# A three-layer block on one core with its opening rebuilt: squares and seven modulation slabs on TensorE, the shift added into FFN 0's operand, filter arithmetic on VectorE, another load order

## The chip, the cores and the metric

One core of one Trainium2 chip. The engines are TensorE (PE, its weight loads PEld), VectorE (DVE), ScalarE (ACT), GpSimd (POOL) and SyncE (SP), which issues nearly all loads. The metric is the device time of one execution in microseconds, of which the median of the runs is given. Rows of the trace count from the start of the span of the one profiled execution.

## The reference

A sequence of 256 tokens of width 1024 passes two layers and a third one of another kind. Each of the first two is an FFN, a mixer and a second FFN, and each of these three has a shift, a gain and a gate that come from a conditioning vector c through a matrix of 1024 by 9216:

```python
cond = jax.nn.silu(c)
for l in range(DEPTH):
    m = (cond @ w_mod[l] + b_mod[l]).reshape(bsz, 3, 3, D_MODEL)
    x = x + 0.5 * m[:, 0, 2][:, None] * swiglu(adaln_in(x, norm_g[l, 0], m, 0), ...)   # FFN 0
    h = adaln_in(x, norm_g[l, 1], m, 1) @ w_in[l]
    ...                                   # mixer_ab (layer 0), mixer_cd (layer 1)
    x = x + m[:, 1, 2][:, None] * (mix @ w_out[l])
    x = x + 0.5 * m[:, 2, 2][:, None] * swiglu(adaln_in(x, norm_g[l, 2], m, 2), ...)
def adaln_in(x, g, m, i):
    return rmsnorm(x, g) * (1 + m[:, i, 1][:, None]) + m[:, i, 0][:, None]
```

`mixer_cd` in layer 1 needs the spectrum of a long filter: three small layers of 64 with a sine, a product with `f_w4`, a decay, and a transform of 512 points. It depends on no token, so it can be computed at any time before layer 1's mixer. Layer 0 needs none of it.

## The kernel before

Everything is fp32. x lies in SBUF with the 1024 features on partitions, as 8 pieces of 128 x 256 tokens. A large product is done with each operand split in a rounded high part and a low part (fp32r), so one 128x128 block costs three matmuls: high by high, high by low, low by high. A slab is one 128 x 1024 piece of weights (512 KB): 8 blocks, 24 matmuls, 128 outputs for 256 tokens. FFN 0 reads 43 slabs of its first two matrices (the first three together, block by block, as x's pieces come), then 22 slabs for the projection down.

Weights and the modulation matrix come in one stream of 512 KB loads, in the order of the list `order`: `("w", i)` is a weight slab, `("m", i)` a modulation slab. They land in a ring of 6 buffers (u_75 to u_80); a load waits until the work that read its buffer is done. For a weight slab ACT rounds the high part and VectorE subtracts it to get the low part, into a ring of 5 pairs (u_81/u_82 to u_89/u_90). For a modulation slab VectorE multiplies 128 rows by the silu of c (`condb`, c repeated on all partitions) and sums each row: one column of `mods` (u_70). Slabs 0 to 7 hold the gain of layer 0's FFN 0, slabs 8 to 15 its shift. In the kernel before slabs 8 to 11 are instead laid out for TensorE (`PE_GROUPS`): products with a weight of one column, 512 columns streamed, a copy, and four more matmuls that turn the row into columns.

The order on each engine is written by a planner: jobs ask for an engine, and the one that can start soonest by its own costs is placed next, with penalties (`HPEN` for the filter's job, `RPEN`, `MPEN`, ...). What is in an engine's queue then runs strictly in that order. Tiles of one program differ by number (u_127 to u_129: PSUM of the slabs; u_130 to u_134: PSUM for the rest; u_68, u_69: high and low part of the normalised x).

The opening before: c is spread over partitions by two matmuls; x's squares are made by ACT, added up by POOL and summed over partitions by TensorE (`Norm.square`, `Norm.root`); then a reciprocal root of eight small VectorE operations (`rsqrt`), a spread over partitions by TensorE (`spread`), and `normalise`: x times gain times root, split in high and low part. FFN 0's shift rides along as two further columns of the operand (258 instead of 256), filled by `shift_cols`, and is added as a bias when a slab is read out (`done`). `hyena_spectrum` runs beside all this, with its additions on POOL (`reduce_angle`, `tap_sums`). The jobs of the opening have to end before the mixer of layer 0 begins: `main` waits for `bg` after FFN 0.

Of the kernel before, what the change touches and what calls it, by code (L numbers as in the profile page):

```python
# [11 lines left out]
F32 = mybir.dt.float32  # L12
# [3 lines left out]
ALU = mybir.AluOpType  # L16
# [4 lines left out]
P = 128  # L21
# [114 lines left out]
PE_GROUPS = (2,)  # L136
# [4 lines left out]
def _pack(inp):  # L141
# [79 lines left out]
    for l in range(2):  # L221
        m = np.ascontiguousarray(inp["w_mod"][l].T).reshape(9, 8, P, 1024)
        m = m[M_SECS].reshape(18, 4, P, 1024)
        if l == 0:
            for g in PE_GROUPS:
                o = M_SECS[g // 2] * D + g % 2 * 512
                m[g] = inp["w_mod"][0][:, o:o + 512].reshape(4, 2, P, 512).transpose(0, 2, 1, 3).reshape(4, P, 1024)
        ms.append(m.reshape(72, P, 1024))
# [67 lines left out]
EX = (2, 3, 8)  # L296
DRATE, DLAT = 350.0, 1.3
HPEN = -0.6
# [178 lines left out]
def _body(tc, ins, out, ctx, dbg=None):  # L477
# [74 lines left out]
    order = [("m", i) for i in range(12)] + [("w", 0)] + [("m", i) for i in range(12, 16)]  # L552
    mi, credit = 16, 0.0
    for i in range(NW):
        if i:
            order.append(("w", i))
# [8 lines left out]
    m_ev = {(l, s): Event() for l in range(2) for s in range(9)}  # L565
    cond_ev, x_ev = Event(), Event()
# [31 lines left out]
    def lo_job():  # L598
        for oi, (kind, i) in enumerate(order):
# [11 lines left out]
            elif i // 4 in PE_GROUPS:  # L611
                continue
            else:
# [8 lines left out]
                mod_done(l, M_SECS[r // 8], 1)  # L622
# [4 lines left out]
    def mod_done(l, s, n):  # L627
        m_left[l, s] = m_left.get((l, s), 8) - n
        if m_left[l, s] == 0:
            fire(m_ev[l, s])  # L630


    def pe_mod(g, ccol, one1, row):
        c0 = M_SECS[g // 2] * 8 + g % 2 * 4
        yield cond_ev
        b, = yield chb, 1
        for i in range(4):
            oi = order.index(("m", 4 * g + i))
            yield raw_ev[oi]
            yield "pe"  # L640
            for e in range(2):
                k = 2 * i + e
                pe.matmul(b[0:1], ccol[:, k:k + 1], raw_t[oi][:, 512 * e:512 * e + 512], start=(k == 0), stop=(k == 7))
            put(raws, raw_t.pop(oi))
        yield "act"
        act.activation(row, b[0:1], AF.Copy)
        put(chb, b)
        b, = yield chb, 1
        yield "pe"
        for j in range(4):  # L650
            pe.matmul(b[:, j:j + 1], row[:, j * P:j * P + P], one1[:, 0:1], start=True, stop=True)
        yield "dve"
        dve.tensor_tensor(mods[0][:, c0:c0 + 4], b[:, :4], V("b_mod", c0, 4), ALU.add)
        put(chb, b)
        mod_done(0, M_SECS[g // 2], 4)
# [140 lines left out]
    class Norm:  # L796
        def __init__(self, A, h, lo, width=D):
# [5 lines left out]
            self.adder = ("dve", dve)  # L803
# [17 lines left out]
        def normalise(self, k, src):  # L821
# [4 lines left out]
            yield from split(self.h[:, k, :T], self.lo[:, k, :T], t, self.need(k))  # L826
            put(sc, t)
            self.use()
# [7 lines left out]
        def square(self, src):  # L836
# [5 lines left out]
            else:  # L842
                yield self.adder[0]
                self.adder[1].tensor_tensor(self.acc, self.acc, s, ALU.add)
# [5 lines left out]
        def root(self):  # L850
            b, = yield chb, 1
            r, = yield sm, 1
            if self.rows:
                self.rstd, = yield sc, 1
# [3 lines left out]
            put(sc, self.acc)  # L858
            yield from rsqrt(r[:, :2], b[:, :2], self.width, sm, (chb, b))
# [87 lines left out]
    def ffn(l, i, nm, nxt):  # L947
        with tc.tile_pool(name=f"ffn{l}{i}", bufs=1) as sp:
# [5 lines left out]

            def done(s, ps):
                t, = yield sc, 1
                b, = yield sm, 1
                if nm.whole:
                    h = ps[:, :T]
                    yield "act"  # L960
                    act.activation(b[:, 0:1], ps[:, T:T + 1], AF.Copy)
                else:
                    h = t
                    yield from evict(nm, t, b[:, 0:1], ps)
                j = s // 2
                if s == 42:
# [4 lines left out]
                    if nm.whole:  # L971
                        put(mmr, ps)
# [5 lines left out]
                elif s % 2 == 0:  # L978
                    yield "act"
                    act.activation(t, h, AF.Silu, bias=b[:, 0:1])  # L980
                    if nm.whole:
                        put(mmr, ps)
# [1362 lines left out]
```

## Time and profile before

| what | value |
|---|---|
| runs of the kernel before | 1431.0, 1426.72, 1430.66 us; median 1430.66 us |
| profiled execution | 1425.9 us, of which the span is 1424.0 us |
| PE busy, share of the span | 1375.6 us, 97% |
| VectorE, ScalarE, GpSimd | 80%, 55%, 3% |
| FFN 0's slabs begin | first matmul at 55.35 us, without larger gaps from 57.74 us |

The busy shares are means over the whole span. In the opening PE has gaps, while behind it the matmuls follow each other almost without one. A PE time in a row of matmuls is modelled at its end; the start of the next weight load or matmul is the surer mark.

### The profile page before, as it was taken

To read this page: it belongs to the slowest core of one execution; us is meant where nothing else is said; L and a number is where in the kernel's file an instruction comes from. 1 tells how busy PE (TensorE), PEld (TensorE's weight loads), DVE (VectorE), ACT (ScalarE), POOL (GpSimd) and SP (SyncE) were. 2 spreads that over 40 slices of the span, in tenths; PEclk is the share of its full clock that TensorE was granted. 3 is DMA by queue.
4 is the path that set the end of the run, shared out by engine and by line. 5 is a ranking of instruction groups with operands and counts; after the bars stand their busy time and mean duration, and the time that the engine had idled before them with its cause. 6 is when DMAs were issued, how large, how long until landed. Compare 5 with 4: busy or idle time off the path is not lost.

```text
span 1424.0 us, 26962 instructions
## 1 busy us (share of the span) xinstructions
PE 1375.6 (97%) x10726; PEld 1292.5 (91%) x10726; DVE 1141.8 (80%) x2183; ACT 778.2 (55%) x1434; POOL 40.9 (3%) x44
## 2 busy tenths in 40 slices
PE   5899999999999999999999999999999999999998
PEld 1499999878999999999998789999998779899998
DVE  5788788796888777888979879986577878799962
ACT  2365554474555544555447646655455765576642
POOL 5200000000000000000000001000000000000000
PEclk9999999999999999999999999999998999899999
DMA  8678889754787776888974447676643244366671
GB/s 296 220 252 315 290 311 326 241 160 152 248 264 249 239 246 226 299 272 279 343 283 152 158 146 231 221 253 184 192 143 107 72 130 138 90 184 186 193 228 54
DMA packets 84655, 305.25 MB, mean 214 GB/s; under 512 B 9515, under 2 KB 11147, under 8 KB 84274
## 3 DMA queue, kind: packets, MB, share of 16 engines
q1 hardware_dynamic: 83250, 299.31, 64.5%
q0 software_dynamic: 1280, 4.22, 0.9%
q8 instruction: 84, 1.38, 0.4%
q14 instruction: 41, 0.34, 0.1%
HBM read 302.43 MB, written 1.06 MB: 213 GB/s over the span
## 4 chain that ended last, share of the span: by engine, by line
PE 84%; DVE 7%; ACT 5%; DMA 1%; POOL 1%; issue 1%; SPq 0%; ACTq 0%; DVEq 0%; POOLq 0%
PE u L445 84%; DVE u L445 7%; ACT u L445 4%; POOL u L445 1%; DMA u<-wst 1%; DMA u<-x 1%; ACT L445 0%; SPq L572 0%; POOL u L2151 0%; ACTq L445 0%; DVEq L445 0%; DVE u L1655 0%; DVE u L1159 0%; DVE u L1656 0%; DVEq L1159 0%
## 5 line engine op out<-in xcount | busy, mean ns | idle before, releaser
L445 PE MATMUL u<-u,u 128*128 128x258 f32 (+7 forms) x10724 | 1374.5, 292 | 44.7 <-ACT u L445 24.2
L445 PEld LDWEIGHTS u<-u,u 128*128 128x128 f32 (+3 forms) x10724 | 1292.2, 189 | 126.1 <-issue 50.3
L445 ACT ACTIVATE u<-u 128x1024 fp32r<-128x1024 f32 (+6 forms) x1001 | 603.1, 632 | 534.0 <-PE u L445 311.3
L445 DVE TENSOR_TENSOR u<-u,u 128x1024 fp32r<-128x1024 f32 (+5 forms) x1065 | 734.0, 721 | 181.0 <-ACT u L445 91.9
L445 DVE SCALAR_TENSOR_TENSOR u<-u,u,u 128x256 f32<-128x256 f32 (+2 forms) x393 | 185.6, 481 | 65.2 <-PE u L445 34.2
L445 ACT ACTIVATE u<-u,u 128x256 f32<-128x256 f32 (+2 forms) x323 | 165.3, 523 | 85.6 <-DVE u L445 61.0
L445 DVE CUSTOM_DVE_ANT_0 u<-u,u,u 128x1024 f32<-128x1024 f32 x140 | 179.9, 1287 | 3.8 <-DMA u<-mst 3.7
L445 DVE SCALAR_TENSOR_TENSOR u<-u,u 128x2 f32<-128x2 f32 (+5 forms) x127 | 32.5, 261 | 13.3 <-ACT u L445 5.6
L445 ACT ACTIVATE u<-u,u,u 128x256 f32<-128x256 f32 (+1 forms) x43 | 23.8, 564 | 8.3 <-DVE u L445 5.7
L445 DVE TENSOR_SCALAR u<-u,u 128x256 f32<-128x256 f32 (+1 forms) x80 | 25.8, 370 | 1.6 <-ACT u L445 0.8
L445 DVE TENSOR_SCALAR u<-u 128x2 f32<-128x2 f32 (+9 forms) x82 | 14.9, 184 | 7.2 <-PE u L445 3.7
L445 POOL TENSOR_TENSOR u<-u,u 128x256 f32<-128x256 f32 (+1 forms) x10 | 14.5, 1448 | 12.3 <-ACT u L445 11.9
L445 DVE TENSOR_REDUCE u<-u 128x2 f32<-128x512 f32 x20 | 13.3, 683 | 1.9 <-PE u L445 1.9
L445 ACT ACT_TABLE_LOAD x11 | 14.1, 1283 | 0.9 <-PEq L2322 0.7
L1338 POOL DMA_DIRECT2D u<-rope x1 | 0.5, 548 | 480.0 <-PE u L445 480.0
L445 POOL TENSOR_SCALAR u<-u 64x256 f32<-64x256 f32 (+2 forms) x12 | 12.7, 1055 | 24.5 <-DVE u L445 18.4
L445 DVE DVE_READ_ACCUMULATOR2_ANT u<- 128x1 f32 x156 | 12.7, 82 | 0.0
L445 ACT ACTIVATION_READ_ACCUMULATOR u<-u,u,u 128x1 f32 x40 | 8.2, 205 | 0.0
L445 DVE TENSOR_TENSOR u<-u 128x2 f32<-128x2 f32 (+5 forms) x36 | 6.7, 189 | 0.6
L1153 POOL DMA_DIRECT2D u<-sel x1 | 0.6, 578 | 192.9 <-DMA u<-mst 192.9
L445 DVE CUSTOM_DVE_ANT_0 u<-u,u 128x256 f32<-128x256 f32 x16 | 6.0, 420 | 0.0
L445 DVE TENSOR_TENSOR_SCAN u<-u,u 128x256 f32<-128x256 f32 x8 | 5.4, 680 | 0.0
(35 smaller groups left out, 25.8 us busy)
## 6 DMA issues: line engine op xcount, KB each, us to landing
u<-wst SPq DMA_DIRECT2D x417, 512.0 KB, 4.5
u<-mst SPq DMA_DIRECT2D x144, 512.0 KB, 4.8
u<-u POOLq DMA_DIRECT2D x1, 1536.0 KB, 10.8
u<-x SPq DMA_DIRECT2D x1, 1024.0 KB, 8.2
u<-mem SPq DMA_DIRECT2D x1, 1024.0 KB
u<-lruw POOLq DMA_DIRECT2D x2, 512.0 KB, 4.3
out<-u SPq DMA_DIRECT2D x8, 128.0 KB, 3.3
u<-decay SPq DMA_DIRECT2D x1, 512.0 KB, 8.3
```

Source lines behind the costliest of these rows:

```text
L445: r = f(*args, **kw)
L1153: nc.gpsimd.dma_start(sel, ins["sel6"][:8, :4 * P])
L1338: nc.gpsimd.dma_start(rope, ins["rope"])
```

## The change

The edit does seven things in the opening. (1) Seven of the first 16 modulation slabs (1, 3, 5 of the gain; 8, 10, 12, 14 of the shift) go to TensorE, each as eight matmuls of 128x128 weights on one column of silu(c); ACT adds the bias as it reads the sum out. (2) x's squares are summed by TensorE: 8 pieces by 2 halves of the tokens, 16 matmuls with one column each. (3) c is loaded already repeated on 128 partitions. (4) FFN 0's shift is added when x is normalised, so that FFN 0 works on 256 columns and its read-out has no bias; the eight shift slabs each release one piece of x. (5) The filter's additions move from POOL to VectorE. (6) The load order: x after two modulation slabs instead of three, the filter's constants before slab 4, weight slabs 0 to 2 between slabs 8 and 12. (7) The planner's penalty for the filter job goes from -0.6 to 0.3.

```diff
-PE_GROUPS = (2,)
+PE_SLABS = (1, 3, 5, 8, 10, 12, 14)
-EX = (2, 3, 8)
+EX = (0, 2, 4)
-HPEN = -0.6
+HPEN = 0.3
-    order = [("m", i) for i in range(12)] + [("w", 0)] + [("m", i) for i in range(12, 16)]
+    order = [("m", i) for i in range(9)]
+    for i in range(3):
+        order += [("w", i), ("m", 9 + i)]
+    order += [("m", i) for i in range(12, 16)]
...
+    def pe_mod(i, ccol):
+        c = M_SECS[i // 8] * 8 + i % 8
+        oi = order.index(("m", i))
         yield cond_ev
+        yield raw_ev[oi]
         b, = yield chb, 1
         yield "pe"
+        for k in range(8):
+            pe.matmul(b[:, 0:1], raw_t[oi][:, k * P:k * P + P], ccol[:, k:k + 1], start=(k == 0), stop=(k == 7))
+        put(raws, raw_t.pop(oi))
+        yield "act"
+        act.activation(mods[0][:, c:c + 1], b[:, 0:1], AF.Identity, bias=V("b_mod", c))
...
-        def normalise(self, k, src):
+        def normalise(self, k, src, shift, ev):
             yield self.done
             t, = yield sc, 1
             yield "dve"
             dve.scalar_tensor_tensor(t, src, self.A[:, k:k + 1], self.rstd, ALU.mult, ALU.mult)
-            yield from split(self.h[:, k, :T], self.lo[:, k, :T], t, self.need(k))
+            self.use()
+            yield ev
+            h = self.h[:, k, :T]
+            yield "act"
+            act.activation(h, t, AF.Identity, bias=shift)
+            yield "dve"
+            dve.scalar_tensor_tensor(self.lo[:, k, :T], t, shift, h.bitcast(F32), ALU.add, ALU.subtract)
...
+        def sums(self, src):
+            b, = yield chb, 1
+            for k in range(8):
...
+                act.activation(s, src[:, k], AF.Square)
+                pe.matmul(b[:, 0:1], s[:, :P], ones[:, 0:1], start=(k == 0), stop=(k == 7))
+            for k in range(8):
+                pe.matmul(b[:, 1:2], sq[k][:, P:], ones[:, 0:1], start=(k == 0), stop=(k == 7))
...
-            yield from shift_mod(l, 2 * i)
-            yield from slab_mms(43, xh, xl, T + 2, done, nm.kev())
+            if nm.whole:
+                yield from slab_mms(43, xh, xl, T, done_whole, nm.kev(), parts=[(k,) for k in range(8)])
+            else:
...
-        yield "pool"
+        yield "dve"
...
-            load(crow[0:1], ins["c"], 4)
+            load(condb, bass.AP(ins["c"].tensor, ins["c"].offset, [[0, P], [1, D]]), 524)
```

`done_whole` is `done` without the bias column and its copy; a slab's sum is read straight from PSUM. `slab_mms` now goes through the first three slabs one block of x at a time.

How the queues move is seen at three places. On TensorE before FFN 0, the kernel before (u_77 to u_80 are modulation slabs 8 to 11, u_247 is the filter's last weights, u_169 the filter, u_148 the transform's matrix):

```order
L445 MATMUL u_133<-u_65,u_93 128x1 x2
L445 MATMUL u_134<-u_77,u_63 1x512 x2
L445 MATMUL u_130<-u_247,u_91 128x512
L445 MATMUL u_132<-u_65,u_104 128x128 x2
L445 MATMUL u_131<-u_247,u_91 128x512
L445 MATMUL u_134<-u_78,u_63 1x512 x2
...
L445 MATMUL u_131<-u_150,u_149 128x1 x4
L445 MATMUL u_132<-u_169,u_148 128x512 x2
L445 MATMUL u_133<-u_169,u_148 128x512 x2
L445 MATMUL u_134<-u_169,u_148 128x512 x2
```

and the changed kernel at the same place (u_63 is silu(c), u_75 to u_80 slabs, u_65 the column of ones, u_93 to u_102 squares of x, u_309 the filter's last weights, u_81 the first weight slab):

```order
L445 MATMUL u_134<-u_63,u_80 128x1 x8
L445 MATMUL u_131<-u_65,u_99 128x1
L445 MATMUL u_130<-u_63,u_77 128x1 x8
L445 MATMUL u_131<-u_65,u_100 128x1
L445 MATMUL u_132<-u_92,u_150 64x256
...
L445 MATMUL u_134<-u_63,u_78 128x1 x8
L445 MATMUL u_130<-u_63,u_80 128x1 x8
L445 MATMUL u_133<-u_65,u_105 128x128 x2
L445 MATMUL u_132<-u_309,u_91 128x512
L445 MATMUL u_127<-u_68,u_81 128x256
L445 MATMUL u_127<-u_69,u_81 128x256
```

Before FFN 0 there now stand 56 matmuls of slabs and 16 of squares, and only one of the filter's 14 products of 512 columns.

On TensorE between FFN 0 and the mixer, the kernel before (u_176 is the low part of FFN 0's inner result, u_127<-u_68 the mixer's first slab):

```order
L445 MATMUL u_129<-u_175,u_90 128x256
L445 MATMUL u_129<-u_175,u_89 128x256
L445 MATMUL u_127<-u_68,u_81 128x258
L445 MATMUL u_127<-u_69,u_81 128x258
L445 MATMUL u_127<-u_68,u_82 128x258
```

and the changed kernel (u_170 the filter, u_148 the transform's matrix, u_171 the squared filter, u_96 and u_110 the sum of squares and the root of the mixer's norm):

```order
L445 MATMUL u_129<-u_176,u_90 128x256
L445 MATMUL u_134<-u_309,u_91 128x512
L445 MATMUL u_130<-u_65,u_96 128x1 x2
L445 MATMUL u_133<-u_309,u_91 128x512
L445 MATMUL u_132<-u_65,u_110 128x128 x2
L445 MATMUL u_131<-u_170,u_148 128x512 x2
L445 MATMUL u_130<-u_170,u_148 128x512
L445 MATMUL u_134<-u_65,u_171 128x1 x4
...
L445 MATMUL u_133<-u_170,u_148 128x512 x2
L445 MATMUL u_131<-u_170,u_148 1x512 x2
L445 MATMUL u_127<-u_68,u_81 128x258
```

The filter's transform, its tap sums and two of the four products before it have moved from the opening to the seam between FFN 0 and the mixer; one more product stands at the start of FFN 0's projection down.

On VectorE ahead of FFN 0, the changed kernel (ISA u_75, u_76, u_79 are modulation slabs 15, 16, 17; u_88 is the low part of weight slab 3; u_67 is x, u_104 the gain, u_98 the spread root):

```order
L445 ISA u_75,u_70<-u_75,u_142,u_63 128x1024
L445 ISA u_76,u_70<-u_76,u_142,u_63 128x1024
L445 TENSOR_TENSOR u_88<-u_77,u_87 128x1024
L445 ISA u_79,u_70<-u_79,u_142,u_63 128x1024
L445 SCALAR_TENSOR_TENSOR u_93<-u_67,u_104,u_98 128x256
L445 SCALAR_TENSOR_TENSOR u_94<-u_67,u_104,u_98 128x256
...
L445 SCALAR_TENSOR_TENSOR u_102<-u_67,u_104,u_98 128x256
L445 SCALAR_TENSOR_TENSOR u_69<-u_93,u_70,u_68 128x256
L445 SCALAR_TENSOR_TENSOR u_69<-u_94,u_70,u_68 128x256
```

All eight products of x come before the first low part, and two slabs of later sections and a weight slab come before them.

## Rows read from the trace of the kernel before

**Rows 1.** Page, part 1: busy time (share of the span) and instructions of each engine.
```profile
PE 1375.6 (97%) x10726; PEld 1292.5 (91%) x10726; DVE 1141.8 (80%) x2183; ACT 778.2 (55%) x1434; POOL 40.9 (3%) x44
```

**Rows 2.** Waits of PE from 62 us on: total us, times, longest.
```profile
PE u L445 <- DVE u L445: 12.0, 11, 2.3
PE u L445 <- ACT u L445: 9.9, 14, 1.8
```

**Rows 3.** Chain that ended last, 40 to 80 us: start, length, what.
```profile
47.02 10.68 DVE u L445 x15
57.74 13.33 PE u L445 x77
...
71.84 8.28 PE u L445 x67
```

**Rows 4.** DMA up to 62 us: GB/s in 40 equal slices; issues, KB, us to landing.
```profile
GB/s 0 124 210 338 359 410 418 394 418 415 418 325 275 402 423 410 415 394 58 0 0 180 423 74 5 0 233 404 320 172 338 225 103 235 177 372 306 225 256 293
u<-x SPq DMA_DIRECT2D x1, 1024.0 KB, 8.2
```

**Rows 5.** PE by form, 24 to 31 us: operands, shapes, xcount, busy us, mean ns.
```profile
L445 PE MATMUL u<-u,u 128*1 128x512 f32 x4 | 3.6, 1046 | 0.0
L445 PE MATMUL u<-u,u 128*128 128x1 f32 x4 | 1.0, 357 | 3.4 <-POOL u L445 3.4
```

**Rows 6.** Stretches: start:end, length, busy (x) of PE, PEld, DVE, ACT, POOL; PEclk, DMA, GB/s.
```profile
25.40:26.50 1.10, 1.06 (x5) 1.01 (x6) 0.00 (x0) 0.00 (x0) 0.94 (x2) 1.00 1.04 413
56.00:62.00 6.00, 4.26 (x7) 0.87 (x7) 6.00 (x9) 1.58 (x2) 0.00 (x0) 0.50 0.87 266
62.00:64.00 2.00, 2.00 (x15) 2.00 (x15) 0.49 (x3) 0.59 (x1) 0.00 (x0) 0.81 0.94 342
```

**Rows 7.** PE by form, the whole stretch to 62 us.
```profile
L445 PE MATMUL u<-u,u 128*128 128x512 f32 x16 | 7.1, 599 | 0.0
L445 PE MATMUL u<-u,u 64*128 64x512 f32 x8 | 6.4, 886 | 1.1 <-ACT u L445 1.1
L445 PE MATMUL u<-u,u 64*64 64x256 f32 x4 | 2.2, 658 | 10.9 <-ACT u L445 10.9
L445 PE MATMUL u<-u,u 33*8 33x512 f32 x2 | 1.9, 1038 | 0.0
L445 PE MATMUL u<-u,u 128*128 128x128 f32 x4 | 1.2, 462 | 0.0
```

**Rows 8.** VectorE by form, the whole span.
```profile
L445 DVE TENSOR_TENSOR u<-u,u 128x1024 fp32r<-128x1024 f32 x417 | 507.7, 1223 | 78.3 <-ACT u L445 75.5
L445 DVE CUSTOM_DVE_ANT_0 u<-u,u,u 128x1024 f32<-128x1024 f32 x140 | 179.9, 1287 | 3.8 <-DMA u<-mst 3.7
L445 DVE SCALAR_TENSOR_TENSOR u<-u,u,u 128x256 f32<-128x256 f32 x306 | 145.8, 485 | 51.9 <-PE u L445 31.9 <-ACT u L445 18.9 <-issue 0.5
L445 DVE TENSOR_TENSOR u<-u,u 128x512 f32<-128x512 f32 x4 | 2.8, 692 | 2.8 <-PE u L445 2.8
```

**Rows 9.** ScalarE by form, the whole span.
```profile
L445 ACT ACTIVATE u<-u 128x1024 fp32r<-128x1024 f32 x417 | 438.6, 1056 | 283.2 <-PE u L445 202.6 <-DMA u<-wst 46.7 <-ACT u L445 19.7
L445 ACT ACTIVATE u<-u 128x512 f32<-128x512 f32 x31 | 18.0, 603 | 6.7 <-PE u L445 5.2 <-POOL u L445 1.3
```

**Rows 10.** Stretches of slabs with 258 columns (FFN 0) and with 256 (last FFN).
```profile
100.00:160.00 60.00, 60.00 (x505) 60.00 (x504) 50.24 (x71) 33.21 (x65) 0.00 (x0) 1.00 0.91 314
1255.00:1345.00 90.00, 90.00 (x774) 90.00 (x773) 85.64 (x162) 61.39 (x97) 0.00 (x0) 1.00 0.62 188
```

**Rows 11.** Timeline of the seam FFN 0 to mixer: start, length, engine, operation, xcount, [idle before].
```profile
248.88 9.67 PE L445 MATMUL u<-u,u 128*128 128x258 f32 x79 [0.66 <-DVE u L445]
251.91 0.36 DVE L445 TENSOR_SCALAR u<-u 128x2 f32<-128x2 f32 x2
252.90 0.55 DVE L445 SCALAR_TENSOR_TENSOR u<-u,u 128x2 f32<-128x2 f32 x3
```

**Rows 12.** PE by form, 1200 to 1210 us.
```profile
L445 PE MATMUL u<-u,u 128*128 128x1 f32 x16 | 2.0, 229 | 0.0
```

**Rows 13.** POOL by form, to 62 us.
```profile
L445 POOL TENSOR_TENSOR u<-u,u 128x512 f32<-128x512 f32 x3 | 5.5, 1828 | 8.3 <-ACT u L445 8.3
```

More of the change, by code (lines that the diff above doesn't have):

```diff
@@ L222, in _pack @@
         m = np.ascontiguousarray(inp["w_mod"][l].T).reshape(9, 8, P, 1024)
-        m = m[M_SECS].reshape(18, 4, P, 1024)
+        m = m[M_SECS].reshape(72, P, 1024)
         if l == 0:
[L225 to L228, printed above, removed]
+            for i in PE_SLABS:
+                o = M_SECS[i // 8] * D + i % 8 * P
+                m[i] = slabs(inp["w_mod"][0][:, o:o + P])[0]
+        ms.append(m)
     out["mst"] = np.concatenate(ms)
@@ L565, in _body @@
     m_ev = {(l, s): Event() for l in range(2) for s in range(9)}
+    slab_ev = [Event() for _ in range(16)]
     cond_ev, x_ev = Event(), Event()
@@ L621, in lo_job, with mod_done @@
                     op0=ALU.mult, op1=ALU.add, accum_out=mods[l][:, c:c + 1])
-                mod_done(l, M_SECS[r // 8], 1)
+                mod_done(i)
             put(raws, raw_t.pop(oi))
     m_left = {}
[L627 to L634, printed above, removed]
-        yield cond_ev
[L636 to L647, printed above, removed]
+    def mod_done(i):
+        key = i // 72, M_SECS[i % 72 // 8]
+        m_left[key] = m_left.get(key, 8) - 1
+        if i < 16:
+            fire(slab_ev[i])
+        if m_left[key] == 0:
+            fire(m_ev[key])
+    def pe_mod(i, ccol):
+        c = M_SECS[i // 8] * 8 + i % 8
+        oi = order.index(("m", i))
+        yield cond_ev
+        yield raw_ev[oi]
         b, = yield chb, 1
         yield "pe"
[L650 to L653, printed above, removed]
+        for k in range(8):
[3 more added lines that the diff above has]
+        act.activation(mods[0][:, c:c + 1], b[:, 0:1], AF.Identity, bias=V("b_mod", c))
         put(chb, b)
-        mod_done(0, M_SECS[g // 2], 4)
+        mod_done(i)
     def tune(name):
@@ L952, in ffn, with done_whole @@
             sl = {}
+            def done_whole(s, ps):
+                t, = yield sc, 1
+                h = ps[:, :T]
+                j = s // 2
+                if s == 42:
+                    h3, = yield sc, 1
+                    yield "act"
+                    act.activation(h3[:64], h[64:], AF.Copy)
+                    act.activation(t[:64], h[:64], AF.Silu)
+                    put(mmr, ps)
+                    yield "dve"
+                    dve.tensor_tensor(t[:64], t[:64], h3[:64], ALU.mult)
+                    put(sc, h3)
+                    yield from split(gh[:64, j], gh[64:, j], t[:64], kev[j])
+                elif s % 2 == 0:
+                    yield "act"
+                    act.activation(t, h, AF.Silu)
+                    put(mmr, ps)
+                    sl[j] = t
+                    fire(st[j])
+                    return
+                else:
+                    yield st[j]
+                    yield "dve"
+                    dve.tensor_tensor(t, h, sl[j], ALU.mult)
+                    put(mmr, ps)
+                    put(sc, sl.pop(j))
+                    yield from split(gh[:, j], gl[:, j], t, kev[j])
+                put(sc, t)
             def done(s, ps):
@@ L957, in done @@
                 b, = yield sm, 1
[L958 to L964, printed above, removed]
+                h = t
+                yield from evict(nm, t, b[:, 0:1], ps)
                 j = s // 2
@@ L1621, in tap_sums @@
             if i:
-                yield "pool"
-                pool.tensor_tensor(sq[0], sq[0], sq[1], ALU.add)
+                yield "dve"
+                dve.tensor_tensor(sq[0], sq[0], sq[1], ALU.add)
         b, = yield chb, 1
@@ L2232, in cond @@
                 yield c_ev
[L2233 to L2236 removed]
                 yield "act"
[L2238 to L2239 removed]
+                act.activation(condb, condb, AF.Silu)
                 act.activation(ccol, ccol, AF.Silu)
[L2241 removed]
                 fire(cond_ev)
             spawn(cond())
[L2245 to L2246 removed]
+            for i in PE_SLABS:
+                spawn(pe_mod(i, ccol))
             spawn(hi_job(), urgency(0))
```

86 lines of the change are left out of this document (40 added, 46 removed).

## The prediction

> **What bounds the kernel now.** I read the page's busy shares first: PE is busy for 97% of the span [rows 1]. Then PE's waits from 62 us on: 12.0 and 9.9 us, some 22 us of 1362 [rows 2]. So behind the opening the program is a row of matmuls, and a microsecond that TensorE gains or loses anywhere comes out at the end. Next the chain through the opening [rows 3]: VectorE for 10.7 us from 47.02, matmuls from 57.74, and at 71.84 the first matmul of FFN 0's slab 3, after the first three slabs. From that mark on matmuls follow each other without a gap. I therefore sum four things: when that mark comes in the changed kernel, what the slabs after it cost, what is new inside FFN 0, and what is new at its end.
>
> **The opening.** The edit puts on TensorE, ahead of FFN 0, 56 matmuls of slabs and 16 of squares, each 128x128 weights on one column. Two of this kind (four records) stand in the trace of before: 1.0 us of PE [rows 5], with PE and its loads busy for all of 25.4 to 26.5 [rows 6]: 0.50 us each. In a dense part of the program 16 records took 2.0 us [rows 12]: 0.25 us. The difference is the clock: passes of 512 columns took 1046 and 886 ns in the opening [rows 5, 7] and 7.1/16 = 0.44 us later [rows 7], so the opening ran at the 1.2 GHz level although its rows print a granted 1.00 [rows 6]; a granted 0.50 stands in the page only for 56 to 62, after TensorE had been mostly idle.
>
> I take 0.50 for all 72, as it is what this very matmul took in the opening; the dense part's 0.25 comes from behind a long row of large matmuls. That is 36 us. With them stand the one-hot product (2 x 1.04 = 2.1), three filter layers (2 x 0.66 each, 3.9), the spread (1.2) and one product of the filter (2 x 0.89 = 1.8) [rows 7]: 45 us in one queue. It starts when slab 1 has landed: 1.9 MB lie ahead and with it, which the slices reach near 8.2 us, and x landed at 4.2 + 8.2 = 12.4, 1.4 us after its 3 MB had flowed [rows 4]; so about 9.5. TensorE's queue then ends at 54.5. Loads do not set this: 13.2 MB up to slab 15 take until 36 at the 415 GB/s of the slices [rows 4]. They are held back, though, since weight slab 1 waits for slab 5's buffer, and that for TensorE.
>
> The spread ends 1.8 earlier, at 52.7. Then in VectorE's order come eight products of x (8 x 0.485 = 3.9 [rows 8], with 0.4 for the copy of the root) and only then the first low part: 57.0 + 0.5 = 57.5. TensorE's second matmul in FFN 0 waits for that, and all that follows. 72 matmuls at 118.8 ns [rows 10] are 8.6 us, and the first 4.7 at half speed cost 2.3 more (before: from 57.74 to about 62.4 [rows 3, 6]). Slab 3 starts at 68.5 instead of 71.84: 3.3 us gained. Bounds: 21.3 gained where only the loads count (rival 1), and 1.2 where ScalarE's roundings of two weight slabs (1.06 each [rows 9]) come ahead of x's first high part.
>
> The remaining edits are paid under this queue. Repeating c on load adds 0.5 MB, 1.3 us at 415 GB/s, and takes two matmuls out. The filter's 64x256 operations on VectorE cost under 0.5 us each (a 128x256 one with three operands takes 0.485 [rows 8]), some 12 of them; VectorE waits for TensorE there, and without that cover they would cost some 4 us. The adds of 128x512 took 1.83 on POOL [rows 13] and should take 0.69 on VectorE [rows 8].
>
> **The slabs.** With 258 columns 505 matmuls took 60 us, with 256 774 took 90 [rows 10]: 118.8 against 116.3 ns. Slabs 3 to 42 have 40 x 24 matmuls: 2.4 us gained; bounds 0.8 (two columns at 2.4 GHz) and 2.8.
>
> **Inside FFN 0.** One product of the filter at the start of the projection down: two passes at 0.44 [rows 7], 0.9 us lost, on a PE without gaps.
>
> **The seam to the mixer.** Here before loses 0.66 us: PE waits for the shift columns [rows 11]. Now the tail of the filter's job stands in TensorE's queue between FFN 0's last matmul and the mixer's first. Its work alone is 2 products, 8 matmuls of the transform and 2 for one row, each two passes of 0.44, 10.6 us, and 4 tap sums at 0.25, 1.0 [rows 7, 12]: 11.6, the lower bound. But it is a chain in strict order. From the last matmul of FFN 0 (248.2) to the end of the norm's root (253.4) took 5.2 us in before [rows 11]; the spread now stands in TensorE's queue ahead of the transform, so 0.6 for it gives 5.8. Three matmuls of the transform follow (to 8.5). Then the tap sums, which wait for ScalarE and VectorE in turn: spread copied 0.4, four squares at 0.60 [rows 9], three adds at 0.69 [rows 8], gaps of some 0.07, thus 5.4: until 11.3. Tap sums 1.0, seven matmuls 6.2: 18.5. Then ScalarE copies the last row (0.6), and the mixer's shift columns stand behind that copy in its queue: 19.5. Less the 0.66 of before and 1.0 for the root's sums and the spread, which leave the mixer's stream: 17.8 us lost. Nothing hides it, since the mixer's slabs all come later in TensorE's queue. Bounds: 10.6 (its work less 1.0) and 22 (the gaps let the clock fall for the first transforms).
>
> **The sum.** -3.3 - 2.4 + 0.9 + 17.8 = +13.0 us on the profiled execution's 1425.9: 1438.9. That execution lies 4.8 below the median of the three runs, of which one (1426.72) is as fast; I keep 1439 and leave the rest to the range. The change breaks even where the opening gains 16.3 us, that is, where slab 3 starts at 55.5.
>
> **The rivals.** The first two rest on TensorE's small matmuls at 0.25 us after the first few: 18 us less in its queue. For it speaks that this queue now runs without pause from 9.5 on; against it that TensorE stayed at 886 and 1046 ns through the busy pieces of the opening [rows 5, 7].
>
> The Trainium skill ("TensorE: Matmul & The Clock Gate", Part 1: The HAM clock gate) says that the throttled clock is the default and that a monitor of how busy the array has been releases it; whether small matmuls behind large weight loads count as busy, no run here shows. By this rule the clock would be up and the next two cases would hold. The same page (Part 2, LDWEIGHTS) prices a weight load by its columns at 1.2 GHz, an estimate of 0.11 us a record for 128; the record here takes 0.25 us at the low clock [rows 6], so the measurement decides, and by the page's price the queue would be 20 us shorter and again the next two cases would hold.
>
> Rival 1, the loads alone set the opening, and it ends faster: slab 15 flows until 36, lands by 37.4, its sum takes 1.36 with its read, then product, high part, low part: FFN 0 runs from 42, slab 3 at 50.5. 21.3 gained: 1425.9 - 21.3 + 16.3 = 1420.9. It decides from a slab 3 before 55.5. Against it: VectorE's queue has two slabs of later sections and a weight slab ahead of the first product of x.
>
> Rival 2, VectorE's queue sets it, no change: slab 17's buffer comes free by slab 13's sum, near 37, and its data lands at 41.5 or later. In order then the sums of slabs 15 to 17 and one low part (1.29 and 1.22 each [rows 8]), until 44.4; eight products 3.9, a low part: 48.9. With 8.6 and 1 for the clock slab 3 starts at 58.5: 13.3 gained, 1428.9.
>
> Rival 3, the seam costs 22 because TensorE is idle in it more than it works at first, and the clock falls as it did at 56 [rows 6]: 1443.
>
> **Chances.** Forecast 0.56; rival 1 0.13; rival 2 0.24; rival 3 0.07. A measurement of this kernel tells about 0.3% (4.3 us) from no change. Faster: rival 1 and a little of rival 2, 0.16. Within: most of rival 2 and an edge of the forecast, 0.23. Slower: 0.61. The range reaches from just below rival 2 to rival 3 with the runs' own 4 us: 1426 to 1446; the forecast's own is 1433 to 1445.
>
> **What would show it.** The trace after should show slab 3's first matmul near 68 (before 55.5 contradicts the opening); records of 128x1 near 0.25 us each in the opening (0.125 would be rivals 1 and 2); 116 ns per matmul in FFN 0; and between FFN 0's last matmul and the mixer's first some 19 us with PE idle for 6 to 8 of them, waiting for ScalarE and VectorE at the tap sums. If that stretch is under 14 us, or the opening gains over 16, the sign of the forecast is wrong.

## The result, and the profile after

The changed kernel takes 1435.91 us (median of 13 runs, 1429.27 to 1443.51), the kernel before, run beside it, 1429.39 us (13 runs). The ratio is 1.0062, with a 95% interval of 1.0044 to 1.0081: slower by 0.6%. The profiled execution after has a span of 1429.9 us against 1424.0. The page's first part, which answers to [rows 1], looks as full as before; the 0.6% that decide here can't be seen in it:

```profile
PE 1388.7 (97%) x10838; PEld 1316.4 (92%) x10838; DVE 1134.7 (79%) x2193; ACT 772.9 (54%) x1395; POOL 8.2 (1%) x18
```

The chain of waits through the opening, after (start us, length us, what), answers to [rows 3]:

```profile
3.35 5.97 DMA u<-mst
...
9.45 11.88 PE u L445 x42
...
22.28 24.97 PE u L445 x112
47.27 0.39 ACT u L445
47.69 3.67 DVE u L445 x9
51.40 38.64 PE u L445 x315
```

The opening is now TensorE's queue: from 9.45, when slab 1 has landed, to 47.25, where the spread ends, then its copy and eight products of x with a low part on VectorE, and from 51.40 matmuls without a gap. What stands in that queue, by form, to 57 us after (operands, shapes, xcount, busy us, mean ns of a record, idle before), answers to [rows 5, 7]:

```profile
L445 PE MATMUL u<-u,u 128*128 128x1 f32 x144 | 31.6, 353 | 9.9 <-DMA u<-mst 9.5 <-ACT u L445 0.4
```

These are the 72 small matmuls, two records each: 31.6 us, 0.44 us each, and a record's mean of 353 ns is that of the opening before (357), not the 229 of the dense part [rows 5, 12]. The granted clock prints 1.00 in this stretch, as it did before; experiment 5 shows what that is worth. ScalarE's row of the first slab's read-out, after:

```profile
60.86 5.06 ACT L445 ACTIVATE u<-u 128x256 f32<-128x256 f32 x8 [9.07 <-PE u L445]
```

Before, ScalarE began that first read-out at 71.09, with the bias column:

```profile
71.09 0.17 ACT L445 ACTIVATE u<-u 128x1 f32<-128x1 f32 x1 [8.37 <-PE u L445]
71.30 0.47 ACT L445 ACTIVATE u<-u,u 128x256 f32<-128x256 f32 x1
```

So the opening gained 10.2 us by this mark; by slab 3's first matmul (71.8 before, 61.4 after) it is 10.4.

The two stretches that answer to [rows 10] (start:end, length, PE busy and records, granted clock, DMA share, GB/s):

```profile
100.00:160.00 60.00, 60.00 (x517) 1.00 0.87 292
1260.00:1350.00 90.00, 90.00 (x774) 1.00 0.63 193
```

FFN 0 now does 517 matmuls in 60 us where it did 505: 116.1 ns instead of 118.8, the rate of the last FFN. Last, the seam from FFN 0 to the mixer, after: TensorE's waits in the timeline, which answer to [rows 11], and the chain through them:

```profile
238.55 8.17 PE L445 MATMUL u<-u,u 128*128 128x1 f32 x16 [1.46 <-DVE u L445]
247.32 7.26 PE L445 MATMUL u<-u,u 128*128 128x1 f32 x22 [0.59 <-DVE u L445]
255.42 9.01 PE L445 MATMUL u<-u,u 128*128 128x258 f32 x72 [0.84 <-ACT u L445]
```

```profile
224.98 11.08 PE u L445 x94
236.08 2.43 DVE u L445 x5
238.55 3.77 PE u L445 x10
242.35 1.43 ACT u L445 x3
243.80 0.70 DVE u L445
...
246.57 0.70 DVE u L445
247.32 7.28 PE u L445 x22
...
255.42 6.61 PE u L445 x52
```

FFN 0 ends at 236.06, the root of the norm follows on VectorE, the spread and one transform on TensorE, the tap sums' squares and additions in turn on ScalarE and VectorE (242.35 to 247.27), the rest of the transform, and at 255.42 the mixer begins: 19.4 us, of which before had 0.66.

| stretch, from the two traces | before | after | difference |
|---|---|---|---|
| start to first slab read out | 71.09 | 60.86 | -10.2 |
| from there to FFN 0's last matmul | 177.1 | 175.2 | -1.9 |
| from there to the mixer's first matmul | 0.66 | 19.4 | +18.7 |
| from there to the end of the span | 1175.1 | 1174.5 | -0.6 |
| span | 1424.0 | 1429.9 | +5.9 |

### The profile page after: what moved, and what is told of

The parts are those of the page before. It is cut to its first block, busy times and chain, and to the rows that moved or that the text cites. A ratio compares the mean times of both kernels' runs of the same rounds, so it can differ in the third digit from the quotient of the medians.

```text
span 1429.9 us, 27171 instructions
## 1 busy us (share of the span) xinstructions
PE 1388.7 (97%) x10838; PEld 1316.4 (92%) x10838; DVE 1134.7 (79%) x2193; ACT 772.9 (54%) x1395; POOL 8.2 (1%) x18
## 4 chain that ended last, share of the span: by engine, by line
PE 86%; DVE 7%; ACT 4%; DMA 1%; issue 1%; SPq 0%; ACTq 0%; DVEq 0%
PE u L445 86%; DVE u L445 7%; ACT u L445 4%; DMA u<-wst 1%; DMA u<-mst 0%; ACT L445 0%; SPq L576 0%; ACTq L445 0%; DVEq L445 0%; DVE u L1701 0%; DVE u L1702 0%; DVE u L1703 0%; DVE u L1387 0%
## 5 line engine op out<-in xcount | busy, mean ns | idle before, releaser
L445 PE MATMUL u<-u,u 128*128 128x256 f32 (+5 forms) x10836 | 1387.7, 292 | 38.0 <-DVE u L445 16.6
L445 PEld LDWEIGHTS u<-u,u 128*128 128x128 f32 (+1 forms) x10836 | 1316.1, 191 | 110.0 <-issue 49.0
L445 DVE TENSOR_TENSOR u<-u,u 128x256 f32<-128x256 f32 (+5 forms) x1079 | 739.6, 716 | 195.9 <-ACT u L445 103.0
L445 DVE SCALAR_TENSOR_TENSOR u<-u,u,u 128x256 f32<-128x256 f32 (+2 forms) x380 | 177.0, 477 | 54.5 <-PE u L445 34.1
L445 ACT ACTIVATE u<-u,u 128x256 f32<-128x256 f32 (+3 forms) x315 | 159.1, 520 | 98.3 <-DVE u L445 60.5
L445 DVE CUSTOM_DVE_ANT_0 u<-u,u,u 128x1024 f32<-128x1024 f32 x137 | 174.9, 1277 | 7.6 <-DMA u<-mst 7.6
L445 DVE SCALAR_TENSOR_TENSOR u<-u,u 128x2 f32<-128x2 f32 (+5 forms) x127 | 28.5, 230 | 8.5 <-ACT u L445 6.0
L445 DVE TENSOR_SCALAR u<-u 128x8 f32<-128x8 f32 (+9 forms) x94 | 18.2, 194 | 13.2 <-PE u L445 4.5
L445 DVE TENSOR_TENSOR u<-u 128x2 f32<-128x2 f32 (+7 forms) x39 | 8.8, 227 | 0.7
L445 DVE SCALAR_TENSOR_TENSOR u<-u 128x2 f32<-128x2 f32 (+3 forms) x24 | 3.9, 163 | 0.7
```

Source lines behind the costliest of these rows:

```text
L445: r = f(*args, **kw)
```

## The experiments

Two marks are read in each trace: the first slab read out (the opening's end, 60.86 in the changed kernel) and the mixer's first matmul (255.42). From there on every run has the same matmuls (with a late filter, the eight records of the mixer's norm fall ahead of the mark), in the same order for 820 us; behind that the planner's order differs from run to run. That rest took between 1168.9 and 1183.5 us, and the granted clock stood at 0.50 for 27.6 us of the shortest (experiment 2) and 51.7 of the longest (8). So places and prices are read at the marks, and which version is faster from the ratios. "Before" ran beside each.

**1. The filter back in the opening.**

```diff
-HPEN = 0.3
+HPEN = -0.6
```

> The changed kernel with the filter's products, transform and tap sums back in the opening (rank -0.6), everything else as changed. Theory A (TensorE's queue sets the opening, and its clock is at the lower level there): the 11.6 us of filter work that stand at the seam cost about twice that in the opening, 23 us, and the 18.8 us of the seam go: slab 3's first matmul near 84 instead of 61.6, time about 4 us above the changed kernel's, 1.009 of before. Theory B (the opening's queue has waits in which the filter fits): slab 3 starts near 70, the seam is 0.7 us again, and the time is some 10 us below the changed kernel's, 0.999 of before. Both expect the seam to shrink to under 2 us; if it does not, the filter is not what fills it.

Ratio 1.0056 [1.0036, 1.0076]; first slab read out at 80.86, mixer at 255.47 with TensorE waiting 0.56 there. The opening lost 20.0 us and the seam gave 18.8 back, to 0.1 us at the mixer's mark. Theory A holds in place (slab 3's first matmul starts at 81.4), though the time came out level with the changed kernel's and not 4 us above. The seam is the filter, and in the changed kernel's opening the same work costs no less.

**2. The filter among FFN 0's first slabs.** `HPEN = 0.0`.

> The changed kernel with the filter's job ranked beside FFN 0's first slabs (rank 0.0): two of its products ahead of FFN 0, the rest between the matmuls of its first three slabs. Theory A (the seam costs 18.8 us since the filter is a chain there with nothing beside it; the work alone is about 11 us at full clock, more where the clock is still low): the seam falls to 0.7 us, slab 3 starts 11 to 14 us later than in the changed kernel (61.6), and the time is 5 to 8 us below the changed kernel's, 0.999 to 1.001 of before. Rival B (the chain waits for ScalarE and VectorE as long there as at the seam, because TensorE goes strictly in order): slab 3 starts 19 us later, no difference from the changed kernel, 1.006 of before.

Mixer at 253.83, 1.6 us earlier than in the changed kernel: the place is nearly rival B's, the reason is another. The filter's rows stand there with the slabs' (57 to 80 us; form, busy, mean ns):

```profile
L445 PE MATMUL u<-u,u 128*128 128x256 f32 x74 | 16.2, 361 | 3.1 <-DVE u L445 3.1
L445 PE MATMUL u<-u,u 128*128 128x512 f32 x16 | 9.0, 650 | 0.0
```

TensorE does not wait in these 23 us (its one wait, 3.1 us, ends at 56.94); it works off the filter's passes of 512 columns, 0.43 us apart. Its start is slow besides: a 256-column record behind another one takes 415 ns up to 63.7 us and some 280 later. (The row's 16.2 us also hold the records' overlap with those passes.) The ratio, 1.0005 [0.9987, 1.0024], is better than this mark explains: this run lost 5.6 us less behind the mixer's start, where the clock stood at 0.50 for 27.6 us, in the changed kernel for 34.1, and where TensorE's order differs in places. How the 5.6 divide is open.

**3. Without the filter's tail.** All after the sine layers is removed, and `pool.memset(kspec, 0.0)`, `pool.memset(kgain, 1.0)` stand for it.

> The changed kernel without the filter behind its sine layers (last layer's products, transform, tap sums are left out; the spectrum is set to zero, the gain to one), so that the price of that whole tail is measured. Theory A (the tail is the only thing in the seam): the seam falls to under 2 us and FFN 0 loses its one product of the filter: 19 to 20 us less than the changed kernel, 0.992 of before. Rival B (the seam would be filled by something else that is late, the root of the norm and its spread or the mixer's shift columns): the seam stays at 6 us or more and the gain is 14 us or less, 0.996 of before or above.

Ratio 0.9933 [0.9908, 0.9958], 1.3% under the changed kernel (about 18 us); mixer at 237.66 with a wait of 0.56. Theory A, though the opening came 2.2 us later than the changed kernel's (63.05), unexplained. So the tail's whole price is known, 18 us, and nothing else fills the seam. Whether the tail could wait until layer 1's mixer needs it was not tried.

**4. The kernel before, with only the filter late.**

```diff
-HPEN = -0.6
+HPEN = 0.3
```

> The kernel before with one line changed: the filter's job ranked behind FFN 0 (rank 0.3) as in the changed kernel; slabs, squares, loads and 258 columns stay as before. It splits the changed kernel's opening gain of 10.2 us into the filter's removal and the rest. Theory A (before's opening is set by VectorE's row of sums and squares, so taking the filter out of it gains little there): slab 3's first matmul 0 to 4 us earlier than 71.84, the seam about 19 us, time +15 us or more, 1.010 to 1.014 of before. Rival B (the filter's removal is what shortened the opening): slab 3 near 62, time +9 us, 1.006 of before, as the changed kernel's without its 2.0 us in the slabs.

Theory A falls, and rival B is passed: the first slab is read out at 55.07, 16.0 us earlier than before, with x's squares, all slabs and the loads as before. The two marks:

```profile
55.07 0.17 ACT L445 ACTIVATE u<-u 128x1 f32<-128x1 f32 x1 [7.22 <-PE u L445]
```

```profile
257.55 9.01 PE L445 MATMUL u<-u,u 128*128 128x258 f32 x72 [0.84 <-ACT u L445]
```

The ratio is 1.0039 [1.0023, 1.0055]; the mixer starts 8.7 us later than before, since the seam takes 23.2 us here. Of the changed kernel's 10.2 us in the opening, then, the filter's departure alone brings more than all; the rest of the change gives 5.8 back (5.6 by slab 3's first matmul).

**5. TensorE busy before slab 1 lands.** Four products of zeros, fp32:

```diff
+            zw = tl(sp, [P, 512])
+            nc.vector.memset(zw, 0.0)
...
+                    pe.matmul(b, zw[:, :P], zw, start=True, stop=True)
...
+            spawn(warm(), -5.0)
```

> The changed kernel with four products of 128x512 zeros on TensorE at the very start, while it would wait for slab 1 (until 9.45). It asks whether the 0.44 us of a slab's matmul in the opening is the clock, and whether a busy start lifts it. Theory A (the clock, and dense work at the start lifts it for good): records of 128x1 fall from a mean of 353 ns to about 240, the 72 matmuls end 12 to 15 us earlier, VectorE's queue then sets the start of FFN 0 and slab 3 starts near 54 instead of 61.6; time 6 to 8 us below the changed kernel's, 1.001 of before. Theory B (it is the clock, and the small matmuls themselves keep it down whatever came before): the first of them may be short, but the mean stays above 320 ns, and the time is that of the changed kernel, 1.006. Theory C (not the clock, but the matmul's own delay in the opening): no record is shorter, 1.006.

Ratio 1.0051 [1.0031, 1.0071], opening's end 60.30: theory B. TensorE's stretches (length, busy and records, granted clock) show it:

```profile
5.00:9.00 4.00, 2.62 (x5) 1.00 1.04 364
9.00:12.00 3.00, 2.84 (x16) 0.64 1.00 418
12.00:14.00 2.00, 1.65 (x4) 0.50 1.08 365
...
20.00:30.00 10.00, 9.56 (x43) 0.50 0.97 366
30.00:40.00 10.00, 10.00 (x45) 0.50 0.94 353
```

The first 16 records took 2.9 us: six of them 250 ns or less, and from the eighth on 352 each. The clock fell among them and stayed at 0.50 until FFN 0, with TensorE busy nearly all the time. Ahead of the first one TensorE had waited 1.54 us for slab 1, so what made the clock fall is open; that the queue of small matmuls did not raise it again is shown. From 24 to 44 us 90 records of 128x1 average 352 ns in this run and 352 in the changed kernel, which prints 1.00 there. So that 1.00 is no measurement, and both ran at the 1.2 GHz level.

**6. Streaming columns between the small matmuls.** One bf16 product of 256 zeros ahead of each of the 56:

```diff
+            nc.tensor.matmul(d[:, :256], box_w[0][:, :P], box_w[0], start=True, stop=True)
```

> The changed kernel with a matmul of 256 columns of bf16 zeros ahead of each of the 56 slab matmuls on TensorE (its sum is used by nobody). It keeps the array in columns between the small matmuls. Theory A (the clock is low because one column a matmul is hardly work): after some microseconds the 128x1 records fall to about 240 ns a record, and the added work of 56 x 0.11 = 6 us at the full clock is outweighed by about 12 us less: slab 3 at 55 to 60, time 0 to 6 us below the changed kernel's. Theory B (the clock stays down): 56 x 0.3 = 17 us more in TensorE's queue, slab 3 near 78, 16 us above the changed kernel's, 1.017 of before.

The clock is theory B's, the price is not: TensorE's queue ended at the same 47.3, and the first slab was read at 60.80. By form, to 62 us:

```profile
L445 PE MATMUL u<-u,u 128*128 128x1 f32 x144 | 31.4, 299 | 8.1 <-DMA u<-mst 7.7 <-ACT u L445 0.4
L651 PE MATMUL u<-u 128*128 128x256 bf16 x56 | 21.0, 374 | 1.1 <-DVE u L2192 1.1
...
L445 PE MATMUL u<-u,u 33*8 33x512 f32 x2 | 1.9, 1036 | 0.0
```

The 299 ns are a mean of two kinds: the record right behind an added product takes 212 ns, the others 352, as in the changed kernel. Within each slab, the first as the last, this pattern repeats every 0.453 us, and the untouched forms take what they took in experiment 5 at 0.50 (33x512: 1036 ns). So the clock was at the lower level throughout, although the column prints 1.00. A small matmul without an added product takes 0.427 us from start to start: 256 columns more cost 0.026 us and not 0.3. Streamed columns, then, are not what sets the pace here; what does was not tested. The ratio is nevertheless 1.0110 [1.0086, 1.0135]: the seam grew by 2.7 us (granted clock 0.55 from 240 to 250 us), and 7.5 us more went behind the mixer's start, 7.1 of them in its first 2000 matmuls (255.3 us in the changed kernel), which are the same in the same order: there the clock stood at 0.50 for 17.1 us instead of 3.4.

**7 and 8. The slabs back on VectorE,** with the filter early (7) and at the seam (8). All 16 are summed there, also the four that the kernel before gave to TensorE in its own layout:

```diff
-PE_SLABS = (1, 3, 5, 8, 10, 12, 14)
+PE_SLABS = ()
```

> The changed kernel with the seven slabs summed by VectorE as before, and the filter back in the opening (rank -0.6); what stays of the change are x's squares on TensorE, the shift in FFN 0's operand with 256 columns, the additions on VectorE and the order of the loads. Theory A (TensorE's queue at the low clock sets the opening; in the run with both in it slab 3 started at about 81.6, and the 56 slab matmuls are 56 x 0.44 = 25 us of that): slab 3 at 60 to 66, bounded by VectorE's seven sums more (7 x 1.36 = 9.5 us), the seam 0.6: time 8 to 14 us below the changed kernel's, 0.995 to 0.999 of before, the best so far. Rival B (the filter's chain waits on VectorE in the opening whoever sums the slabs, as in before, 71.84): slab 3 near 71, the time that of before less 2.4 for the columns, 0.998 of before or above.

> The changed kernel with the seven slabs summed by VectorE as before; the filter stays at the seam. It prices the slabs on TensorE alone. Theory A (56 matmuls at 0.44 us, 25 us, are what sets the opening since the filter is out of it; in the run of the kernel before with the filter late slab 3 started at 55.8): slab 3 at 52 to 57, 5 to 9 us less than the changed kernel, 1.000 to 1.003 of before. Rival B (VectorE, with 9.5 us of sums more, comes as late as TensorE did): slab 3 at 61 to 66, the changed kernel's time or up to 4 us more, 1.006 to 1.009 of before.

Run 7 is among the fastest (run 11, below, overlaps with it): 1416.33 us, ratio 0.9930 [0.9909, 0.9952], 10 us under the kernel before and 1.3% under the changed one, a little better than theory A. First slab at 58.87, mixer at 233.48:

```profile
58.87 3.81 ACT L445 ACTIVATE u<-u 128x256 f32<-128x256 f32 x6 [4.08 <-PE u L445]
```

```profile
233.48 9.66 PE L445 MATMUL u<-u,u 128*128 128x258 f32 x79 [0.56 <-DVE u L445]
```

So the experiments lead to a version that beats both kernels. Run 8 gives 1.0059 [1.0039, 1.0080]: its opening ends at 54.18, 6.7 us earlier than the changed kernel's, as theory A said, but its time is that of rival B: from the seam's first wait to the mixer it took 20.12 us where the changed kernel took 16.87, so that the mixer starts only 3.4 us earlier, and behind it 9.0 us more went, 5.7 of them in the first 2000 matmuls, where the clock stood at 0.50 for 17.1 us instead of 3.4. Granted clock in that seam (start:end, length, busy, clock):

```profile
230.00:240.00 10.00, 6.91 (x15) 0.67 0.56 171
240.00:250.00 10.00, 10.00 (x26) 0.81 0.01 2
```

With the changed kernel and experiment 1 they make a square (mixer's first matmul; ratio to before):

| | filter in the opening | filter at the seam |
|---|---|---|
| seven slabs on VectorE | 233.48; 0.9930 [0.9909, 0.9952] | 252.00; 1.0059 [1.0039, 1.0080] |
| seven slabs on TensorE | 255.47; 1.0056 [1.0036, 1.0076] | 255.42; 1.0062 [1.0044, 1.0081] |

Either edit by itself costs 18.5 to 22.0 us at the mark, and the second one costs 0 to 3.4 more once the first is made. With the slabs on VectorE the filter hides in TensorE's queue: VectorE was busy for all of the opening (29.5 of the 30 us from 20 to 50 in run 7) and sets it (the chain that ended last stays on VectorE from 21.1 to 54.0), and the filter moved the first slab by 4.7 us (54.18 to 58.87). With the slabs on TensorE the queue is full and the filter costs 20.

**9. Two slabs on TensorE, filter early.** `PE_SLABS = (1, 3)` in run 7.

> As the run without slabs on TensorE and with the filter early (slabs 54.1 for the second matmul of FFN 0, profiled total 1413.4), but with two of the seven slabs, 1 and 3, on TensorE. There VectorE was busy for all of 20 to 50 us and TensorE for 6.1 of 11 us between 9 and 20 and 7.6 of 10 between 40 and 50. Theory A (VectorE's queue sets the opening there, TensorE has room for 2 x 3.5 us): VectorE is 2 x 1.36 = 2.7 us shorter, second matmul of FFN 0 at 51.5, time 2 to 3 us less than that run, 0.991 of before. Theory B (strict order in TensorE's queue makes the filter's chain later by the 7 us): second matmul at 57 to 61, 3 to 7 us more than that run, 0.995 to 0.998 of before.

Ratio 0.9947 [0.9924, 0.9969]; first slab at 65.58, 6.7 us later than run 7's, mixer at 240.20. TensorE's last wait ahead of that read-out ended at 56.70 instead of 54.09, near theory B's range. (The expectations of 9 to 12 call this mark FFN 0's second matmul; that one had come at 45.4 in run 7 and at 45.2 here.) The other 4 us go with FFN 0's start at a clock of 0.84 and 0.82 (50 to 70 us), where run 7 prints 1.00. By the mixer's mark even two slabs don't fit; the ratio overlaps with run 7's.

**10 to 12. The remaining edits undone one by one, in run 7:** x's squares added on GpSimd as before (10), the loads in the old order (11), the filter's additions on GpSimd (12).

```diff
-                spawn(nm.sums(x))
+                nm.adder = ("pool", pool)
+                for k in range(8):
+                    spawn(nm.square(x[:, k]))
...
```

```diff
-EX = (0, 2, 4)
+EX = (2, 3, 8)
-    order = [("m", i) for i in range(9)]
...
+    order = [("m", i) for i in range(12)] + [("w", 0)] + [("m", i) for i in range(12, 16)]
...
```

```diff
-                yield "dve"
-                dve.tensor_tensor(sq[0], sq[0], sq[1], ALU.add)
+                yield "pool"
+                pool.tensor_tensor(sq[0], sq[0], sq[1], ALU.add)
...
```

> As the run without slabs on TensorE and with the filter early, but with x's squares summed by seven additions on GpSimd and two matmuls as in the kernel before, in place of 16 matmuls. It asks which of the remaining edits brought that run's 12.2 us in the opening (first slab read out at 58.9 against 71.1). Theory A (GpSimd's row of additions, 0.73 us each, and what waits behind it held before's opening): second matmul of FFN 0 at 58 or later, 4 to 10 us more than that run. Rival B (VectorE's queue hides the root anyway: the root ends there about 36 and the products of x start at 41.5): under 1 us of difference, 0.993 of before.

> As the run without slabs on TensorE and with the filter early, but with the order of the loads as in the kernel before (first weight slab behind 12 slabs, x behind three slabs, the filter's tables behind eight). Theory A (the order is what brought the 12.2 us, since x lands 1.4 us and weight slabs 1 and 2 some 6 us earlier in the new one): the second matmul of FFN 0 at 58 to 66 instead of 54.1, 4 to 12 us more than that run, 0.996 to 1.001 of before. Rival B (VectorE's queue, busy from 8 to 54, sets the opening with either order): within 1.5 us of that run, 0.993 of before.

> As the run without slabs on TensorE and with the filter early, but with the filter's additions (angles, table sums, tap sums) on GpSimd as in the kernel before; so every edit of the change that this run keeps is x's squares on TensorE, 256 columns and the order of the loads. In the run it starts from VectorE was busy from 8 to 54 us, and the moved operations are about 7.5 us of that. Theory A (VectorE's queue sets the opening, GpSimd is idle): VectorE's queue is 7.5 us shorter, the second matmul of FFN 0 comes 4 to 7 us earlier than 54.1, the time is 0.988 to 0.991 of before. Rival B (while GpSimd works, VectorE's operations take longer: the 64x256 one with three operands took 839 ns in the kernel before, where GpSimd was busy, and 417 where it was not; and GpSimd's own take two to four times as long, which lengthens the filter's chain): 9 of those at 0.42 us more are 3.8, the sums and low parts another 2 to 3, so nothing is gained: second matmul at 53 to 60, 0.992 to 0.997 of before.

The mixer starts at 238.73, 237.37 and 238.63 instead of 233.48: 5.3, 3.9 and 5.2 us. With the 2.9 that the columns give in run 7 (slab 3's first to FFN 0's last matmul, 176.4 before and 173.5) that is 17.3, and the whole step from before (248.88) to run 7 is 15.4, so each of the four edits carries a part and the parts overlap. (Two smaller ones, c loaded repeated and slabs 8 to 11 on VectorE, were not undone.)

In 12 rival B holds by both of its marks: the last wait ends at 59.11. In 10 the mixer's mark fits theory A and in 11 it lies between the theories, but neither cause is shown: the last wait ends at 54.23 and 46.82, not at 58 or later. In 10 the chain ahead of it holds no GpSimd but a weight slab that lands late (5.12 us from 45.71), and FFN 0 then runs at 0.66 (50 to 60 us); in 11 twelve of the filter's passes stand behind that wait, where run 7 has none.

The ratios, 0.9945 [0.9926, 0.9964], 0.9923 [0.9898, 0.9949] and 0.9961 [0.9942, 0.9980], overlap with run 7's, so by time alone no one of these three is settled. For 12 the rows show the cause that the rival named. VectorE's scalar-tensor-tensor operations by form, to 60 us: run 12, then run 7.

```profile
L445 DVE SCALAR_TENSOR_TENSOR u<-u,u 64x256 f32<-64x256 f32 x9 | 5.8, 640 | 5.1 <-POOL u L445 4.9
L445 DVE SCALAR_TENSOR_TENSOR u<-u,u,u 128x256 f32<-128x256 f32 x8 | 5.4, 730 | 0.6 <-ACT u L445 0.6
```

```profile
L445 DVE SCALAR_TENSOR_TENSOR u<-u,u 64x256 f32<-64x256 f32 x9 | 3.8, 417 | 0.3
...
L445 DVE SCALAR_TENSOR_TENSOR u<-u,u,u 128x256 f32<-128x256 f32 x8 | 3.5, 480 | 0.0
```

With GpSimd at work the same operations take half as long again and VectorE waits 4.9 us for GpSimd besides. Run 10, where GpSimd only adds x's squares, shows it too: 620 ns for the 64x256 operation.

## Why the prediction was right, and where it was not

The direction, the mechanism and the range held: the opening gains less than the seam costs. That 1439 lies only 3.1 us above the measured 1435.91 is in part luck: the sum overshot by 7.1 us (+13.0 for +5.9 on the spans), but it was added to the profiled execution of before, 1425.9, which lies 3.5 under the median of all its runs, 1429.39. Term by term against the traces:

| term | predicted | measured |
|---|---|---|
| opening | -3.3 | -10.2 |
| slabs and the one product | -2.4 + 0.9 | -1.9 |
| seam | +17.8 | +18.7 |
| behind the mixer's start | 0 | -0.6 |
| sum on the spans | +13.0 | +5.9 |

**The opening was mis-sized, by 6.9 us** (7.1 by slab 3's first matmul, 61.4 for 68.5). TensorE started at 9.45 (predicted 9.5), the clock stayed low and the queue set the start, as forecast; but the spread ended at 47.25 and not at 52.7, 5.4 us of it, mostly because a small matmul took 0.44 us and not 0.50. The 0.50 came from two matmuls that stood by themselves in before [rows 5, 6]; the 72 took 31.6 us instead of 36. The way from there to the first low part (4.2 for 4.8) and FFN 0's first 72 matmuls (10.0 for 11.0, to slab 3) were shorter too.

**Rivals 1 and 2 fell with the clock.** They needed 0.25 us; experiments 5 and 6 show that neither a busy start nor added columns brings the small matmuls there for the length of the opening. By the rule quoted in the prediction from the Trainium skill ("TensorE: Matmul & The Clock Gate", Part 1: The HAM clock gate) a busy array is released; here the engine was busy (9.56 and 10.00 of 10 us in experiment 5's rows) and the clock stayed at 0.50, so the row decides.

**The seam was right in its sum.** The chain took 19.4 where 19.5 was summed, and its middle, squares and additions in turn, 4.9 where 5.4 was. One step was wrong: TensorE did not idle for 6 to 8 us there but for 1.46 + 0.59 + 0.84. It worked through the first transforms at half speed (granted 0.71 from 240 to 250), beside that chain, so rival 3's falling clock was there and cost little; in experiments 6 and 8 it lasted 10.2 us instead of 6.8, and their seams took 2.7 and 3.3 us more.

**What the prediction did not ask** is what each edit is worth alone. It summed the new queue as a whole; experiment 4 shows that the filter's departure alone gains 16.0 in the opening, and experiment 8 that the slabs on TensorE cost 6.7 of what could be had (54.18 to 60.86). It also took VectorE's operations at their mean of the whole span (485 ns), and missed that in the opening they are only so short because GpSimd's work is taken away (690 ns before, 482 after).

## What to carry to other kernels

When two edits both load the same in-order queue, run all four combinations before you judge either: here each looks harmless next to the other (0 to 3.4 us), and each alone costs 18.5 to 22.0 us. A price per instruction is read from a row in the stage and in the company where it will run, since two matmuls alone and 72 in a row differed by 12%. And look for the engine whose queue is full in the stage (VectorE here, once the slabs are back) before work is moved to one that seems idle.

## What was not expected of the hardware

- **Small matmuls did not keep the clock up.** In experiment 5 the granted clock fell from 1.00 to 0.50 within the first records of 128x1, with PE busy 2.84 of 3 us, and rose only in FFN 0. In experiment 6 a product of 256 bf16 columns ahead of each small matmul, with PE busy 4.85 of 5 us, left the other forms at the lengths of the lower level (33x512: 1036 ns in both experiments). In the changed kernel, where the trace shows no such fall ahead of FFN 0, the column printed 1.00 for the same durations; so the level is read from them.
- **GpSimd slows VectorE.** In the kernel before, VectorE's 64x256 operation took 839 ns on the mean, in the changed kernel 416 (620 in run 10, with GpSimd on x's squares alone); its slab sums 1366 and 1277, its 128x256 products 690 and 482. The Trainium skill ("SBUF — State Buffer", Who interferes with whom) says that a VectorE instruction with two SBUF inputs contends with a GpSimd one that reads SBUF; the trace agrees. Rows of VectorE to 62 us, before and then after:

```profile
L445 DVE CUSTOM_DVE_ANT_0 u<-u,u,u 128x1024 f32<-128x1024 f32 x14 | 18.9, 1366 | 3.8 <-DMA u<-mst 3.7
L445 DVE SCALAR_TENSOR_TENSOR u<-u,u 64x256 f32<-64x256 f32 x9 | 7.6, 839 | 5.5 <-POOL u L445 5.3
```

```profile
L445 DVE CUSTOM_DVE_ANT_0 u<-u,u,u 128x1024 f32<-128x1024 f32 x11 | 14.0, 1277 | 7.6 <-DMA u<-mst 7.6
...
L445 DVE SCALAR_TENSOR_TENSOR u<-u,u 64x256 f32<-64x256 f32 x9 | 3.7, 416 | 0.3
```

- **The clock also falls later, in one kernel and not in another, under the same instructions.** The mixer 28 us after its start, behind the same 223 records in the same order, in run 7 and then in the kernel before (TensorE, 4 us each):

```profile
261.48:265.48 4.00, 4.00 (x15) 0.68 0.49 175
265.48:269.48 4.00, 4.00 (x15) 0.50 0.42 122
269.48:273.48 4.00, 4.00 (x15) 0.50 0.45 142
```

```profile
276.88:280.88 4.00, 4.00 (x21) 1.00 0.49 175
280.88:284.88 4.00, 4.00 (x27) 1.00 0.54 162
284.88:288.88 4.00, 4.00 (x36) 1.00 0.31 102
```

The rows, which count a record at an edge twice, have 45 matmuls for run 7 in these 12 us and 84 for the kernel before. Such falls, and beyond 820 us the planner's other order, lie behind the 1168.9 to 1183.5 us of the rest: in the six traces where it took 1179.9 us or more the clock stood at 0.50 for 44 to 52 us of it, in the eight others (1177.4 at most) for 27 to 38. What sets the falls off was not found, and they are the limit of what a ratio of 0.3% can say of this kernel.
